# FFN 1 of a hybrid encoder layer on Trainium2: the norm factor moved from the activations to the gates, two more tiles in Strassen pairs, a bias write cut in pieces

## The chip, the cores and the metric

The kernel runs on one core of one Trainium2 chip. The metric is the device time of one launch in microseconds (us), the median of several runs. Beside it stands one profiled execution, of which the hardware profiler gives every instruction with its start and duration. The engines are TensorE (PE, with its weight loads as PEld), VectorE (DVE), ScalarE (ACT), GpSimd (POOL) and SyncE (SP). Each takes its own queue of instructions strictly in order; semaphores tie the queues together.

## The reference, cut to what matters

One layer, 512 tokens, width 1024, FFN width 2816, all float32:

```python
f = swiglu(rms_norm(x, ffn1_pre_g), ffn1_w1, ffn1_w3, ffn1_w2)   # (silu(u @ w1) * (u @ w3)) @ w2
h = x + 0.5 * rms_norm(f, ffn1_post_g)
u = rms_norm(h, mix_pre_g)
...   # RG-LRU branch, sliding-window attention with a relative bias, gates, w_o
h = h + rms_norm(merged @ w_o, mix_post_g)
f = swiglu(rms_norm(h, ffn2_pre_g), ffn2_w1, ffn2_w3, ffn2_w2)
h = h + 0.5 * rms_norm(f, ffn2_post_g)
```

`rms_norm(x, g) = x * r * g` with one factor `r = 1 / sqrt(mean(x^2) + eps)` for each token. The change concerns the first two lines only. The relative bias (16 heads) is needed in the attention, in the middle of the layer.

## The kernel before, in words

**Split products.** Each float32 operand is split into a high part (an ACT copy to fp32r) and a low part (a DVE subtraction), `hi` and `lo` (`split2`, L189; `split_to`, L149, for weights). A product of two split operands is three matmuls, hi·hi, lo·hi and hi·lo, into one PSUM bank. PE does little else than these.

**FFN 1, single tiles.** The 2816 columns of `w1a` and `w3a` are 22 tiles of 128 columns each. For the first `NC1 = 6` tiles a unit (`mm_feat`, L194) takes the eight 128-row pieces of x^T, three matmuls of 128x512 each, 24 in all. x^T is multiplied by the gain `g` alone and split into the tile `uT` (L665, L666). The factor r is not in it: it is computed from x meanwhile (L676 to L686), spread over the partitions by four small matmuls (L700) into `Rb`, and multiplied on each of the two results of a tile when the gate is made: `silu_mul` (L426) is two multiplications by `Rb` (L433, L434), a silu on ACT (L435), and the product (L436).

**FFN 1, pairs.** The other 16 tiles go two at a time through the class `Pairs` (L478): each pair of tiles and each of the two weights is a *job*, a 2x2 block product done with seven half-width block products instead of eight (Strassen's scheme in Winograd's form). A block product is `mm_s` (L466): twelve matmuls of 128x256. For this the weights need sums (`prep(m, 0)`, four POOL instructions L518 to L521) and splits (`prep(m, 1)` to `prep(m, 4)`, an ACT copy and a DVE subtraction each, L191 and L192), and the activations need four blocks and four sums of blocks, `X1`: `b11, b21, b22, t1` to `t4`, each split. Here x^T **with** the factor is used: `norm_x` (L770, L773) makes it with 16 DVE instructions while the single tiles run, `sums` makes the sums, and the splits go into slots or, as soon as the last single tile has read `uT`, into `uT` (L789 to L794). Inside a job, PSUM bank `bu` carries three successive sums: it is copied out by ACT as `q1` (L551) and as `u` (L560), and the next block product adds on top of it, so PE can't go on in `bu` before the ACT copy. The block product with `a22` is run one job later (`last`, L590), after the next job's second product; for a `w1a` job the silus of all four blocks follow there (L593, L594, L595).

The order of a job on PE is: a11·b11 (`bu`), s1·t1 (`bx`), the previous job's a22·t4, s2·t2 (`bu`), a12·b21 (`bc`), s4·b22 (`bx`), s3·t3 (`bu`). While job n runs, `prep` for job n+1 and the sums for n+2 are issued.

**Order of the work.** There is no scheduler. Each engine's queue is the order in which the Python code calls. `later(n, fn)` and `point()` (L175, L179) place work a number of *points* ahead: a point comes after half a unit, after each `mm_s`, and after each two token tiles in the last product. SP issues the weight loads in the order of the list `order`, each into a slot of a shared pool.

**Then** `tok_gemm` (L330) multiplies the 22 hidden tiles by `w2a`; each k-step is 24 matmuls of 128x512. Two broadcasts (`bcast`, L254, POOL queue) bring the gains near its end, and `norms` does the post norm (`post_norm`, L260, with `eps` as a constant), the residual and the next pre norm.

**The bias.** Two small loads on POOL's queue at the start (L651, L652), one matmul (L691), a copy (L693), and one DMA on POOL's queue (L696) that writes each of the 16 rows 128 times to a scratch in DRAM, 3064 KB. It is read back in the attention (L1012).

Of the kernel before, what the change touches and what calls it, by code (L numbers as in the profile page):

```python
# [51 lines left out]
def hybrid_layer(ctx: ExitStack, tc: tile.TileContext, a: dict, out: bass.AP):  # L52
# [32 lines left out]

    cp.tile([P, 176], F32, name="gap")
    sm.tile([P, 256], F32, name="gap2", bufs=1)
# [139 lines left out]
    class Rstd2:  # L227

        def first(self, ss):
            self.b, self.v, self.r, self.e, self.r2 = (small(1, x) for x in ("b", "v", "r", "e", "r2"))
            dve.tensor_scalar(out=self.b, in0=ss[:, 0:1], scalar1=D * EPS, scalar2=None, op0=ALU.add)

# [9 lines left out]
    def rstd4(s4):  # L244

        v, r, e, r2 = (small(NT, x) for x in ("v", "r", "e", "r2"))
        dve.tensor_scalar(out=v, in0=s4, scalar1=D * EPS, scalar2=None, op0=ALU.add)
        act.activation(r, v, AF.Abs_reciprocal_sqrt)
        dve.tensor_tensor(out=e, in0=r, in1=r, op=ALU.mult)
        dve.tensor_tensor(out=e, in0=e, in1=v, op=ALU.mult)  # L250
        dve.scalar_tensor_tensor(out=r2, in0=e, scalar=-3.0, in1=r, op0=ALU.add, op1=ALU.mult)
        return r2, r

# [5 lines left out]

    def post_norm(acc, t, gpost, scale, dst, after=None, last=False):  # L260

# [5 lines left out]
        for n, c in enumerate(cs):  # L267
            act.activation(junk[:, c], acc[n], AF.Square, accum_out=ss[:, n : n + 1])
            if n:
                rs.root(ss)  # L270
            dve.scalar_tensor_tensor(out=fg[:, c], in0=acc[n], scalar=scale, in1=gpost[:, c], op0=ALU.mult, op1=ALU.mult)
            if not n:
                rs.first(ss)
        r = rs.value()
# [6 lines left out]

    def norms(acc, t, gpost, scale, gpre, spill):

# [10 lines left out]

        post_norm(acc, t, gpost, scale * NEWT, h[t], half)
        if spill:
# [32 lines left out]

    def tok_gemm(nm, xs, n, R, gpost_name, scale, gpre_name, first, x_to=None, xf=None, spill=False, then=None):  # L330

# [36 lines left out]
        gpre = bcast(gpre_name) if gpre_name else None  # L368
        us, trs = {}, {}
        split_to(st["get"] + len(first))  # L370
        dma_to(st["split"] + 2)
        for t in range(NT):
# [15 lines left out]
            if t == NT - 2:  # L388

                transpose_out(trs[t - 1], t - 1)  # L390
            us[t] = norms(acc[t], t, gpost, scale, gpre, spill)
            if t == NT - 2 and xf:
# [7 lines left out]
        for i, key in enumerate(first):  # L400
# [11 lines left out]
            if i == 0:  # L412
                trs[t - 1] = transpose_mm(us[t - 1])
                us[t] = norms(acc[t], t, gpost, scale, gpre, spill)
                transpose_out(trs[t - 1], t - 1)
# [22 lines left out]

    class Hidden:


        def __init__(self):
            self.f, self.t, self.done = [], {}, 0
# [34 lines left out]
    class Pairs:  # L478

        def __init__(self, na, nb, f0, X, hid):
# [52 lines left out]
        def run(self, tail, hooks={}):  # L535
# [4 lines left out]
            for n, (nm, f) in enumerate(self.jobs):  # L540
# [49 lines left out]
                def last(W=W, bu=bu, c=c, f=f, first=first):  # L590
                    mm_s(W.pop("a22"), X["t4"], bu, True)
                    if first:
                        act.activation(c[:, 1, :256], bu, AF.Silu)  # L593
# [6 lines left out]

            last()


# [36 lines left out]
    dma_to(NS + 2)  # L640
    h_load([a["x"][t * P : (t + 1) * P, :] for t in range(NT)])

    hid, X1 = Hidden(), {}
    pairs_a = Pairs("w1a", "w3a", NC1, X1, hid)
    dma_one(pairs_a.k0)
# [29 lines left out]
    del raw3, pair3, hi, lo  # L675
    split_to(NS + 2)  # L676
    s4 = small(NT, "s4")
    for t in range(NT):
        junk = slot([P, D], name="junk")
        act.activation(junk, h[t], AF.Square, accum_out=s4[:, t : t + 1])  # L680

    r, q = rstd4(s4)
    act.activation(tiny, q, AF.Silu)
    dgs = slot([P, NT, P], name="dgs")
    for t in range(NT):
        dve.tensor_scalar(out=dgs[:, t, :], in0=ident, scalar1=r[:, t : t + 1], scalar2=NEWT, op0=ALU.mult, op1=ALU.mult)  # L686
    pairs_a.prep(0, 0, dve)
    ps.append(unit("w3a", 1))

    pse = bank("e")  # L690
    pe.matmul(pse[:N_HEADS, : NREL + 1], oh[:, NREL + 1 :], oh[:, : NREL + 1], start=True, stop=True)  # L691
    erow = slot([N_HEADS, NREL + 1], name="erow")
    act.activation(erow, pse[:N_HEADS, : NREL + 1], AF.Copy)  # L693
    scr = tc.dram_tile([N_HEADS, P, NREL], F32, name="bias_scr")
    ev = erow[:, :NREL]
    pool.dma_start(out=scr, in_=bass.AP(tensor=ev.tensor, offset=ev.offset, ap=[ev.ap[0], [0, P], ev.ap[1]]))  # L696
    Rb = slot([P, SEQ], name="Rb")
    psr = bank("r")
    for t in range(NT):
        pe.matmul(psr[:, t * P : (t + 1) * P], ones, dgs[:, t, :], start=True, stop=True)  # L700
    act.activation(Rb, psr, AF.Copy)
    pairs_a.prep(0, 1)
    hid.f += [silu_mul(ps[0], ps[1], Rb), silu_mul(ps[2], ps[3], Rb)]
    pairs_a.prep(0, 2)
    later(1, lambda: pairs_a.prep(0, 3))
    later(2, lambda: pairs_a.prep(0, 4))

# [27 lines left out]

    def swiglu_units(na, nb, f0, f1, hid, R=None):
        for f in range(f0, f1):
            p1, p3 = unit(na, f), unit(nb, f)
            later(1, lambda p1=p1, p3=p3: hid.f.append(silu_mul(p1, p3, R)))

    def uview(hh, th):
# [3 lines left out]
    def pair_view(p):  # L745
        return lambda e, k: p[e][:, k, :]

    def sums(xf):

        t = [slot([P, 4, 256], name="T") for _ in range(4)]  # L750
        pool.tensor_tensor(out=t[2], in0=xf[1, 1], in1=xf[0, 1], op=ALU.subtract)
        dve.tensor_tensor(out=t[0], in0=xf[0, 1], in1=xf[0, 0], op=ALU.subtract)
        dve.tensor_tensor(out=t[1], in0=xf[1, 1], in1=t[0], op=ALU.subtract)
        dve.tensor_tensor(out=t[3], in0=xf[1, 0], in1=t[1], op=ALU.subtract)
        return t

# [11 lines left out]
    xn, tn = {(hh, th): slot([P, 4, 256], name="xn") for hh in range(2) for th in range(2)}, []  # L768
# [8 lines left out]
    for k in range(KT):  # L777
        later(2 + k // 2, lambda k=k: norm_x(k))
    later(6, lambda: xts.clear())
    later(6, lambda: tn.extend(sums(xn)))  # L780
    later(7, lambda: X1.update(b11=to_slots(xn[0, 0])))
    later(9, lambda: X1.update(t1=to_slots(tn[0])))
    later(11, lambda: X1.update(t2=to_slots(tn[1])))
    end = 2 * 2 * (NC1 - 2)
    for i, at_ in enumerate((end - 5, end - 2, end - 1)):
        later(at_, lambda i=i: pairs_a.prep(1, i))
    swiglu_units("w1a", "w3a", 2, NC1, hid, Rb)
    point(True)
    X1["b21"] = to_uT(xn[1, 0], 1, 0)  # L789

    late = {
        (0, 1): [lambda: X1.update(b22=to_uT(xn[1, 1], 1, 1))],
        (0, 2): [lambda: X1.update(t3=to_uT(tn[2], 0, 1))],
        (0, 3): [lambda: X1.update(t4=to_uT(tn[3], 0, 0)), tn.clear, xn.clear],  # L794
    }

# [410 lines left out]

NC1 = 6
NC2 = 2
# [54 lines left out]
```

## Time and profile before

| | us |
|---|---|
| median of 3 runs (lowest, highest) | 1135.44 (1135.13, 1135.78) |
| the profiled execution's own time | 1135.67 |
| its span, first to last instruction | 1133.8 |
| first matmul of the paired stage of FFN 1 | 74.1 |
| first matmul of w2 of FFN 1 | 235.4 |

The span and the time differ by 1.87 us of work around it. The profiled execution lies 0.23 us above the median. In all tables "busy" is the time that an engine executes, and "idle before" is its wait ahead of an instruction with what ended it.

### The profile page before, as it was taken

To read this page: it belongs to the slowest core of one execution; us is meant where nothing else is said; L and a number is where in the kernel's file an instruction comes from. 1 tells how busy PE (TensorE), PEld (TensorE's weight loads), DVE (VectorE), ACT (ScalarE), POOL (GpSimd) and SP (SyncE) were. 2 spreads that over 40 slices of the span, in tenths; PEclk is the share of its full clock that TensorE was granted. 3 is DMA by queue.
4 is the path that set the end of the run, shared out by engine and by line. 5 is a ranking of instruction groups with operands and counts; after the bars stand their busy time and mean duration, and the time that the engine had idled before them with its cause. 6 is when DMAs were issued, how large, how long until landed. Compare 5 with 4: busy or idle time off the path is not lost.

```text
span 1133.8 us, 17339 instructions
## 1 busy us (share of the span) xinstructions
PE 1125.3 (99%) x6763; PEld 1003.5 (89%) x6763; DVE 790.1 (70%) x1181; ACT 585.2 (52%) x1042; POOL 353.8 (31%) x265
## 2 busy tenths in 40 slices
PE   9999999999999999999999999999999999999997
PEld 7889999988889987888888888889999999998886
DVE  5997889885436747695678865767899777975313
ACT  6445555574324349844655663356555555574211
POOL 0148678500000000001555643000965566700000
PEclk9999999999999999999999999999999999999999
DMA  9953223264313311234122333531323332255101
GB/s 343 157 135 112 93 95 112 76 222 151 110 56 135 144 56 57 75 95 148 56 78 90 93 95 112 185 111 38 113 94 94 112 112 76 94 197 172 40 19 56
DMA packets 36945, 124.94 MB, mean 110 GB/s; under 512 B 4416, under 2 KB 6208, under 8 KB 36864
## 3 DMA queue, kind: packets, MB, share of 16 engines
q1 hardware_dynamic: 34272, 115.15, 30.3%
q0 software_dynamic: 2448, 8.43, 4.0%
q8 instruction: 53, 0.87, 0.3%
q10 hardware_dynamic: 144, 0.26, 0.1%
q14 instruction: 28, 0.23, 0.1%
HBM read 116.50 MB, written 7.33 MB: 109 GB/s over the span
## 4 chain that ended last, share of the span: by engine, by line
PE 93%; DVE 3%; ACT 2%; issue 1%; DMA 0%; SPq 0%; DVEq 0%
PE c L475 11%; PE c L474 11%; PE c L473 11%; PE f L202 10%; PE f L201 10%; PE f L203 10%; PE acc L220 8%; PE acc L221 8%; PE acc L219 8%; PE pt L1067 1%; PE s L1031 1%; PE s L1030 1%; PE tr L310 1%; PE o L1083 1%; PE o L1084 1%
## 5 line engine op out<-in xcount | busy, mean ns | idle before, releaser
L201 PE MATMUL f<-uT,whi 128*128 128x512 f32 (+1 forms) x504 | 184.2, 365 | 0.0
L202 PE MATMUL f<-uT,wlo 128*128 128x512 f32 (+1 forms) x504 | 183.0, 363 | 0.4 <-DVE wlo L157 0.3
L203 PE MATMUL f<-uT,whi 128*128 128x512 f32 (+1 forms) x504 | 182.6, 362 | 0.0
L219 PE MATMUL acc<-whi,hT 128*128 128x512 f32 x352 | 137.1, 390 | 0.0
L220 PE MATMUL acc<-wlo,hT 128*128 128x512 f32 x352 | 137.0, 389 | 0.0
L221 PE MATMUL acc<-whi,hT 128*128 128x512 f32 x352 | 136.9, 389 | 0.0
L474 PE MATMUL c<-Xh,wlo 128*128 128x256 f32 x432 | 122.3, 283 | 0.0
L475 PE MATMUL c<-Xl,whi 128*128 128x256 f32 x432 | 122.3, 283 | 0.0
L473 PE MATMUL c<-uT,whi 128*128 128x256 f32 x432 | 122.3, 283 | 0.0
L474 PE MATMUL c<-uT,wlo 128*128 128x256 f32 x432 | 122.3, 283 | 0.0
L475 PE MATMUL c<-uT,whi 128*128 128x256 f32 x432 | 122.3, 283 | 0.0
L473 PE MATMUL c<-Xh,whi 128*128 128x256 f32 x432 | 122.3, 283 | 0.0
L192 DVE TENSOR_TENSOR wlo<-S,whi 128x1024 fp32r<-128x1024 f32 x72 | 118.2, 1642 | 3.6 <-ACT whi L191 3.2
L202 PEld LDWEIGHTS f<-uT,wlo 128*128 128x128 f32 x504 | 95.2, 189 | 15.8 <-DVE wlo L157 1.6
L201 PEld LDWEIGHTS f<-uT,whi 128*128 128x128 f32 x504 | 95.1, 189 | 15.8 <-issue 1.4
L203 PEld LDWEIGHTS f<-uT,whi 128*128 128x128 f32 x504 | 95.1, 189 | 14.8
L473 PEld LDWEIGHTS c<-Xh,whi 128*128 128x128 f32 x432 | 82.9, 192 | 0.0
L474 PEld LDWEIGHTS c<-Xh,wlo 128*128 128x128 f32 x432 | 82.9, 192 | 0.0
L473 PEld LDWEIGHTS c<-uT,whi 128*128 128x128 f32 x432 | 82.9, 192 | 0.0
L474 PEld LDWEIGHTS c<-uT,wlo 128*128 128x128 f32 x432 | 82.9, 192 | 0.0
L475 PEld LDWEIGHTS c<-uT,whi 128*128 128x128 f32 x432 | 82.9, 192 | 0.0
L475 PEld LDWEIGHTS c<-Xl,whi 128*128 128x128 f32 x432 | 82.9, 192 | 0.0
(309 smaller groups left out, 2703.8 us busy)
## 6 DMA issues: line engine op xcount, KB each, us to landing
raw_w2a<-in_w2a_dram SPq DMA_DIRECT2D x22, 512.0 KB, 3.7
raw_w1b<-in_w1b_dram SPq DMA_DIRECT2D x22, 512.0 KB, 4.2
raw_w3b<-in_w3b_dram SPq DMA_DIRECT2D x22, 512.0 KB, 4.2
raw_w2b<-in_w2b_dram SPq DMA_DIRECT2D x22, 512.0 KB, 4.1
raw_w3a<-in_w3a_dram SPq DMA_DIRECT2D x21, 512.0 KB, 4.5
raw_w1a<-in_w1a_dram SPq DMA_DIRECT2D x20, 512.0 KB, 4.5
raw_wg<-in_wg_dram SPq DMA_DIRECT2D x16, 512.0 KB, 3.7
raw_xr<-in_xr_dram SPq DMA_DIRECT2D x8, 512.0 KB, 4.7
```

Of the source, the lines that this page charges most:

```text
L192: dve.tensor_tensor(out=lo, in0=src, in1=f32(hi), op=ALU.subtract)
L201: pe.matmul(ps[:, c0:c1], wh[:, s], h_, start=k == 0, stop=False)
L202: pe.matmul(ps[:, c0:c1], wl[:, s], h_, start=False, stop=False)
L203: pe.matmul(ps[:, c0:c1], wh[:, s], l_, start=False, stop=k == KT - 1)
L219: pe.matmul(acc[n], x[:, 0, c], wh[:, s], start=first, stop=False)
L220: pe.matmul(acc[n], x[:, 0, c], wl[:, s], start=False, stop=False)
L221: pe.matmul(acc[n], x[:, 1, c], wh[:, s], start=False, stop=last)
L310: pe.transpose(ps[:, k * P : (k + 1) * P], hg[:, kk * P : (kk + 1) * P], ident)
L473: pe.matmul(ps, wh[:, s], xh, start=first, stop=False, skip_group_check=True)
L474: pe.matmul(ps, wl[:, s], xh, start=False, stop=False, skip_group_check=True)
L475: pe.matmul(ps, wh[:, s], xl, start=False, stop=k == 3, skip_group_check=True)
L1030: pe.matmul(o, lq, KS[g][:, 0, k0 : k0 + n], start=True, stop=False)
```

## The change

It makes the paired stage of FFN 1 work on the same unscaled `uT` as the single tiles. Blocks `b11, b21, b22` of `X1` are then plain views of `uT`; only the four sums are made (from `xg`, x^T times g, written by 16 ACT instructions) and split. The factor goes onto the w1 result alone, ahead of the silu; the w3 result stays without it. The hidden tile is then too large by 1/r for each token, which the post norm divides out if its `eps` is multiplied by the same ratio, so `post_norm` takes a column `veps` in place of the constant. `NC1` goes from 6 to 4: tiles 4 and 5 become a ninth pair. The work between is placed anew by hand, and the bias write is cut into eight pieces that are issued during w2.

```diff
-    def post_norm(acc, t, gpost, scale, dst, after=None, last=False):
+    def post_norm(acc, t, gpost, scale, dst, after=None, last=False, eps=D * EPS):
...
         if R is None:
             act.activation(t[:, 0, :], ps1, AF.Silu)
-            dve.tensor_tensor(out=t[:, 1, :], in0=ps3, in1=t[:, 0, :], op=ALU.mult)
         else:
             dve.tensor_tensor(out=t[:, 0, :], in0=ps1, in1=R, op=ALU.mult)
-            dve.tensor_tensor(out=t[:, 1, :], in0=ps3, in1=R, op=ALU.mult)
             act.activation(t[:, 0, :], t[:, 0, :], AF.Silu)
-            dve.tensor_tensor(out=t[:, 1, :], in0=t[:, 1, :], in1=t[:, 0, :], op=ALU.mult)
+        dve.tensor_tensor(out=t[:, 1, :], in0=ps3, in1=t[:, 0, :], op=ALU.mult)
...   # class Pairs, last()
-                    if first:
+                    if first and self.R is not None:
+                        act.activation(c[:, 1, :256], bu, AF.Copy)
+                        dve.tensor_tensor(out=c, in0=c, in1=self.R, op=ALU.mult)
+                        act.activation(c, c, AF.Silu)
+                    elif first:
                         act.activation(c[:, 1, :256], bu, AF.Silu)
                         act.activation(c[:, 0, :], c[:, 0, :], AF.Silu)
                         act.activation(c[:, 1, 256:], c[:, 1, 256:], AF.Silu)
...   # the start
-    oh = slot([N_BUCKETS, NREL + 1 + N_HEADS], name="oh")
-    pool.dma_start(out=oh[:, : NREL + 1], in_=a["onehot"])
-    pool.dma_start(out=oh[:, NREL + 1 :], in_=a["rel_bias"])
+    dma_to(NS + 3)          # one more single tile's load ahead of the first pair's
...
+    def scaled(k):
+        for th in range(2):
+            act.activation(xg[k // 4, th][:, k % 4, :], xts[k // 2][:, k % 2, th * 256 : th * 256 + 256], AF.Copy,
+                           scale=vec[:, V_G1 + k : V_G1 + k + 1])
+    def factor():
+        psr = bank("r")
+        for t in range(NT):
+            pe.matmul(psr[:, t * P : (t + 1) * P], ones, dgs[:, t, :], start=True, stop=True)
+        for i in range(2):
+            act.activation(Rb[:, i, :], psr, AF.Copy)
+    def bias_spread(i):
+        ev = erow[0][2 * i : 2 * i + 2, :NREL]
+        pool.dma_start(out=scr[2 * i : 2 * i + 2], in_=bass.AP(tensor=ev.tensor, offset=ev.offset, ap=[ev.ap[0], [0, P], ev.ap[1]]))
...
-    def norm_x(k):
-        for th in range(2):
-            c = slice(th * 256, th * 256 + 256)
-            dve.scalar_tensor_tensor(
-                out=xn[k // 4, th][:, k % 4, :], in0=xts[k // 2][:, k % 2, c],
-                scalar=vec[:, V_G1 + k : V_G1 + k + 1], in1=Rb[:, c], op0=ALU.mult, op1=ALU.mult)
...
+    X1.update((b, uview(*q)) for b, q in (("b11", (0, 0)), ("b21", (1, 0)), ("b22", (1, 1))))
+    P_ = pairs_a.prep
+    for n, fn in (
+        (1, lambda: t_sum(0)), (1, lambda: t_split(0)), (2, lambda: t_sum(1)),
+        (3, lambda: P_(0, 0, dve)), (3, lambda: t_split(1)), (3, squares), (4, root),
+        (5, lambda: P_(0, 1)), (5, lambda: t_sum(2)), (6, factor), (6, lambda: swiglu(0)), (6, lambda: dma_to(pairs_a.k0 + 4)),
+        (7, lambda: t_sum(3)), (7, lambda: t_split(2)), (8, lambda: P_(0, 2)), (8, lambda: swiglu(1)),
+        (9, lambda: P_(0, 3)), (9, lambda: P_(0, 4)), (10, lambda: t_split(3)), (10, lambda: swiglu(2)),
+        (10, lambda: P_(1, 0, dve)),
+    ):
+        later(n, fn)
...
+    swiglu(3)
+    late = {(6, 1): [bias_in], (9, 1): [bias_rows]}
...
+    for i in range(N_HEADS // 2):
+        later(4 + 3 * i, lambda i=i: bias_spread(i))
     later(10, softplus)
-    bs = tok_gemm("w2a", hid, FT, RF, "ffn1_post_g", 0.5, "mix_pre_g", [("xr", i) for i in range(4)], hid.to, spill=True)
+    bs = tok_gemm("w2a", hid, FT, RF, "ffn1_post_g", 0.5, "mix_pre_g", [("xr", i) for i in range(4)], hid.to, spill=True, eps=veps)
...
-NC1 = 6
+NC1 = 4
```

In the new file these lines stand a few lines lower: the new multiplication of a pair's block by the factor is L597 there, the copy ahead of it L596, the silu L598, and the gate's lines are L436 (factor), L437 (silu), L438 (product).

More of the change, by code (lines that the diff above doesn't have):

```diff
@@ L84, in hybrid_layer @@
     bxh = cp.tile([P, 2, KT], F32, name="bxh")
-    cp.tile([P, 176], F32, name="gap")
+    veps = cp.tile([P, NT], F32, name="veps")
+    cp.tile([P, 172], F32, name="gap")
     sm.tile([P, 256], F32, name="gap2", bufs=1)
@@ L227, in hybrid_layer, with first @@
     class Rstd2:
-        def first(self, ss):
+        def first(self, ss, eps=D * EPS):
             self.b, self.v, self.r, self.e, self.r2 = (small(1, x) for x in ("b", "v", "r", "e", "r2"))
-            dve.tensor_scalar(out=self.b, in0=ss[:, 0:1], scalar1=D * EPS, scalar2=None, op0=ALU.add)
+            dve.tensor_scalar(out=self.b, in0=ss[:, 0:1], scalar1=eps, scalar2=None, op0=ALU.add)
         def root(self, ss):
@@ L251, in rstd4 @@
         dve.scalar_tensor_tensor(out=r2, in0=e, scalar=-3.0, in1=r, op0=ALU.add, op1=ALU.mult)
-        return r2, r
+        dve.tensor_scalar(out=veps, in0=v, scalar1=EPS, scalar2=None, op0=ALU.mult)
+        return r2
     def bcast(name):
@@ L272, in post_norm @@
             if not n:
-                rs.first(ss)
+                rs.first(ss, eps)
         r = rs.value()
@@ L280, in post_norm, with norms @@
                 after(n, c)
-    def norms(acc, t, gpost, scale, gpre, spill):
+    def norms(acc, t, gpost, scale, gpre, spill, eps):
         hg = slot([P, D], name="hg")
@@ L293, in half @@
             dve.scalar_tensor_tensor(out=hg[:, c], in0=h[t][:, c], scalar=NEWT, in1=gpre[:, c], op0=ALU.mult, op1=ALU.mult)
-        post_norm(acc, t, gpost, scale * NEWT, h[t], half)
+        post_norm(acc, t, gpost, scale * NEWT, h[t], half, eps=eps)
         if spill:
@@ L327, in transpose_xf, with tok_gemm @@
             act.activation(xf[half, t // 2][:, :, (t % 2) * P : (t % 2 + 1) * P], v, AF.Copy)
-    def tok_gemm(nm, xs, n, R, gpost_name, scale, gpre_name, first, x_to=None, xf=None, spill=False, then=None):
+    def tok_gemm(nm, xs, n, R, gpost_name, scale, gpre_name, first, x_to=None, xf=None, spill=False, then=None, eps=None):
         F = n - R
@@ L369, in tok_gemm @@
         us, trs = {}, {}
+        ep = lambda t: D * EPS if eps is None else eps[:, t : t + 1]
         split_to(st["get"] + len(first))
@@ L390, in tok_gemm @@
                 transpose_out(trs[t - 1], t - 1)
[L391 removed]
+            us[t] = norms(acc[t], t, gpost, scale, gpre, spill, ep(t))
             if t == NT - 2 and xf:
@@ L675, in hybrid_layer @@
     del raw3, pair3, hi, lo
-    split_to(NS + 2)
-    s4 = small(NT, "s4")
[L678 to L693, printed above, removed]
-    scr = tc.dram_tile([N_HEADS, P, NREL], F32, name="bias_scr")
[L695 to L706, printed above, removed]
+    split_to(NS + 1)
+    xg, tg = {(hh, th): slot([P, 4, 256], name="xg") for hh in range(2) for th in range(2)}, {}
+    def scaled(k):
+        for th in range(2):
+            act.activation(xg[k // 4, th][:, k % 4, :], xts[k // 2][:, k % 2, th * 256 : th * 256 + 256], AF.Copy,
+                           scale=vec[:, V_G1 + k : V_G1 + k + 1])
@@ new lines, in t_sum, with t_split, squares @@
+    def t_sum(n):
+        tg[n] = slot([P, 4, 256], name="T")
+        p, q = ((xg[0, 1], xg[0, 0]), (xg[1, 1], tg.get(0)), (xg[1, 1], xg[0, 1]), (xg[1, 0], tg.get(1)))[n]
+        dve.tensor_tensor(out=tg[n], in0=p, in1=q, op=ALU.subtract)
+    def t_split(n):
+        X1[f"t{n + 1}"] = to_slots(tg[n])
+    dgs = slot([P, NT, P], name="dgs")
+    s4 = small(NT, "s4")
+    def squares():
+        for t in range(NT):
+            junk = slot([P, D], name="junk")
+            act.activation(junk, h[t], AF.Square, accum_out=s4[:, t : t + 1])
@@ new lines, in root @@
+    def root():
+        r = rstd4(s4)
+        act.activation(tiny, tiny, AF.Silu)
+        for t in range(NT):
+            dve.tensor_scalar(out=dgs[:, t, :], in0=ident, scalar1=r[:, t : t + 1], scalar2=NEWT, op0=ALU.mult, op1=ALU.mult)
+    def factor():
+        psr = bank("r")
+        for t in range(NT):
+            pe.matmul(psr[:, t * P : (t + 1) * P], ones, dgs[:, t, :], start=True, stop=True)
+        for i in range(2):
+            act.activation(Rb[:, i, :], psr, AF.Copy)
+    scr = tc.dram_tile([N_HEADS, P, NREL], F32, name="bias_scr")
@@ new lines, in hybrid_layer, with bias_in, bias_rows @@
+    oh, erow = [], []
+    def bias_in():
+        oh.append(slot([N_BUCKETS, NREL + 1 + N_HEADS], name="oh"))
+        pool.dma_start(out=oh[0][:, : NREL + 1], in_=a["onehot"])
+        pool.dma_start(out=oh[0][:, NREL + 1 :], in_=a["rel_bias"])
+    def bias_rows():
+        pse = bank("e")
+        t = oh.pop()
+        pe.matmul(pse[:N_HEADS, : NREL + 1], t[:, NREL + 1 :], t[:, : NREL + 1], start=True, stop=True)
+        erow.append(slot([N_HEADS, NREL + 1], name="erow"))
+        act.activation(erow[0], pse[:N_HEADS, : NREL + 1], AF.Copy)
@@ L734, in softplus @@
                     scalar1=0.5, scalar2=None, op0=ALU.mult)
[L736 to L739, printed above, removed]
     def uview(hh, th):
@@ L746, in pair_view @@
         return lambda e, k: p[e][:, k, :]
[L748 to L755, printed above, removed]
     def to_slots(src):
@@ L765, in to_uT @@
         return uview(hh, th)
-    xn, tn = {(hh, th): slot([P, 4, 256], name="xn") for hh in range(2) for th in range(2)}, []
-    def norm_x(k):
-        for th in range(2):
-            c = slice(th * 256, th * 256 + 256)
-            dve.scalar_tensor_tensor(
-                out=xn[k // 4, th][:, k % 4, :], in0=xts[k // 2][:, k % 2, c],
-                scalar=vec[:, V_G1 + k : V_G1 + k + 1], in1=Rb[:, c], op0=ALU.mult, op1=ALU.mult)
-    for k in range(KT):
-        later(2 + k // 2, lambda k=k: norm_x(k))
@@ L779, in hybrid_layer, with single @@
[L779 to L787, printed above, removed]
-    point(True)
[L789 to L795, printed above, removed]
+    def single(nm, i, ahead):
+        w = get(nm, i, ahead=ahead)
+        ps.append(bank("f"))
+        mm_feat(ps[-1], w)
@@ L797, in w2_ahead @@
+    for k in range(4):
+        scaled(k)
+    split_to(NS + 2)
+    for k in range(4, KT):
+        scaled(k)
+    xts.clear()
+    for u, ahead in zip(order[NS : 2 * NC1], [1] * (2 * NC1 - NS - 1) + [0]):
+        single(*u, ahead)
+    point(True)
+    xg.clear()
+    tg.clear()
+    swiglu(3)
+    late = {(6, 1): [bias_in], (9, 1): [bias_rows]}
     def w2_ahead():
```

12 lines of the change are left out of this document (8 added, 4 removed).

## The prediction

> **What bounds the kernel now.** I read the page's first part, then the waits of PE, then busy time by stage, then the timelines of ACT and DVE around one job of the paired stage.
>
> ```profile
> span 1133.8 us, 17339 instructions
> PE 1125.3 (99%) x6763; PEld 1003.5 (89%) x6763; DVE 790.1 (70%) x1181; ACT 585.2 (52%) x1042; POOL 353.8 (31%) x265
> ```
>
> The waits of PE over the whole span (total, times, longest) are two lines:
>
> ```profile
> PE w L625 <- DVE tiny L629: 1.4, 1, 1.4
> PE f L202 <- DVE wlo L157: 0.3, 1, 0.3
> ```
>
> So PE sets the time, and after the first microseconds it waits for nobody. A change gains what it takes off PE and loses every wait that it gives PE. Busy time by stage (end of the start to the paired stage, then the paired stage):
>
> ```profile
> 30.10:51.90 21.80, 21.80 (x98) 18.03 (x97) 20.73 (x34) 9.40 (x12) 2.83 (x2) 1.00 0.96 136
> 51.90:74.60 22.70, 22.40 (x101) 18.29 (x100) 20.83 (x20) 9.53 (x12) 7.91 (x5) 1.00 0.60 114
> 74.60:246.00 171.40, 171.40 (x1389) 169.59 (x1388) 144.14 (x150) 97.41 (x166) 106.69 (x56) 1.00 0.36 118
> ```
>
> The third number after the stretch is PEld, then come DVE, ACT and POOL. DVE is busy 93% from 30 to 75 us and 84% in the paired stage: it is the engine with no room where the change works. The paired stage of today, ACT first, then DVE:
>
> ```profile
> 84.40 0.38 ACT L551 ACTIVATE ct<-c 128x256 f32<-128x256 f32 x1 [0.54 <-PE c L475]
> ...
> 87.28 0.38 ACT L593 ACTIVATE cc<-c 128x256 f32<-128x256 f32 x1 [1.06 <-PE c L475]
> 87.56 0.62 ACT L594 ACTIVATE cc<-cc 128x512 f32<-128x512 f32 x1
> 88.08 0.41 ACT L595 ACTIVATE cc<-cc 128x256 f32<-128x256 f32 x1
> 88.39 1.05 ACT L191 ACTIVATE whi<-raw_w1a 128x1024 fp32r<-128x1024 f32 x1
> 89.34 0.38 ACT L560 ACTIVATE ct<-c 128x256 f32<-128x256 f32 x1
> ```
>
> ```profile
> 84.20 1.51 DVE L579 TENSOR_TENSOR cc<-ct 128x256 f32<-128x256 f32 x1
> 85.63 1.78 DVE L192 TENSOR_TENSOR w<-raw_w3a,w 128x512 fp32r<-128x512 f32 x1
> ...
> 90.94 2.31 DVE L192 TENSOR_TENSOR wlo<-S,whi 128x1024 fp32r<-128x1024 f32 x1
> ...
> 95.42 0.41 DVE L579 TENSOR_TENSOR cc<-ct 128x256 f32<-128x256 f32 x1
> ...
> 96.69 0.68 DVE L192 TENSOR_TENSOR w<-raw_w1a,w 128x512 fp32r<-128x512 f32 x1
> ```
>
> The same DVE instruction takes 0.41 or 1.51 us, 0.68 or 1.78: 1.1 more when one of POOL's sums, 1.3 us alone, is under way (POOL ran one from 83.27 to 85.43 and from 85.39 to 86.87). POOL's own go from 1.3 to 2.16. The two take turns, whole instructions at a time, wherever DVE reads two SBUF operands.
>
> **PE's own work.** A single unit is 24 matmuls of 128x512; the unit that starts at 22.71 ends its issue 0.2268 us a matmul later, 5.44 in all. A job is 84 matmuls of 128x256; L551 starts at 84.40, 94.48, 104.56: 10.08 a job, 0.120 a matmul, not half of 0.2268, since PEld is full there (169.59 of 171.40). Four units go (21.77), two jobs come (20.16): **1.61 saved**, where the count of columns (21 of 24) would promise 2.7. The bias matmul (0.74) only moves. The first 22.7 us stay, and the loads of w2 and all later stages keep their order.
>
> **The start.** Out go 16 `norm_x` on DVE (0.41 each) and three splits; in come 16 `scaled` copies on ACT (0.40 alone), hidden by 40% of idle ACT before 40 us. The gates lose L434, but it ran while ACT did the silu; without it DVE stands idle in its queue for that time (multiply at 32.90, silu at 33.62, product at 34.29, so 1.99 us a gate, as before). The paired stage now begins after five units instead of nine and the factor's four matmuls (0.92): 22.71 + 3 x 5.44 = 39.04, + 0.92 + 2 x 5.44 = 50.85, 23 us earlier, and its preparation has to be done by then. It is not. The factor is copied 1.2 us after its matmuls begin (28.98 to 30.18) and takes 0.60, so the first gate starts on DVE at about 40.9. From there the built DVE queue holds, up to the multiplication of the fourth gate: three gates (3 x 1.99 = 5.97), six instructions of 1024 columns at 1.14 apart (the low parts of the last single weight, S12, S34, t3 and t4, and the sum t4: 6.84), one of 512 (0.60), four weight sums of job 1 (4 x 0.60 and two hand-offs: 2.6), and two waits for a high part from ACT (0.35 each): 16.7 us. So 57.6; the silu starts 0.7 later. On ACT the copies of gates and jobs stand in one queue: the fourth silu is **ahead of** `q1` of job 0, which therefore is done at 58.3 + 0.53 + 0.38 = 59.2. PE needs `q1` before s2·t2, at 50.85 + 2 x 1.44 = 53.7. PE waits 5.5 us, or 6.7 where POOL's first sums, whose loads no longer meet the bias write, take a turn among the four DVE sums. I take **6.0**. Behind that silu also stands the first split of job 1; it is done two products later, inside PE's next 5.8 us.
>
> **The paired stage.** For each w1 job the three silus (0.38, 0.62, 0.41) become a copy, a DVE multiplication of 1024 columns (L597; L752 is such a one, 1.21) and a silu of 1024 (an ACT copy of that size takes 1.05, 0.95 to the next). Behind them on ACT stand the split of the next weight and `u` (L560), and PE can't begin s3·t3 before `u` is copied. Today `u` is done at 89.72; s3·t3 begins five products after 84.3, at 91.5: 1.8 us of room. With the change: 87.28 + 0.38, hand-off 0.06, DVE 1.22, hand-off 0.06, silu 0.95, split 0.95, copy 0.38 = 91.28. 0.2 us of room is left, if DVE is free and POOL is not in its turn. In today's trace DVE is free at that point of all eight jobs, by as little as 0.3 (w22 ends at 87.41), and POOL is in a sum in four of eight: a wait up to 1.3. Then all splits of the next job come 1.6 to 2 later on ACT; their low parts on DVE have 1.2 of room (the one of S12 ends at 93.25, s1·t1 of that job asks for it at 94.4). So a period of two jobs loses between 0 and 1.3 + 1.2. I walked all nine periods instruction by instruction in the order of the built queues, with these durations and POOL and DVE taking turns: 0.3 to 2.5 each, **11.0** in all. The same walk over the old queues gives PE no wait, as the trace has. With all durations of an engine 3% (POOL 7%) shorter or longer the sum is 8.6 to 14.9.
>
> **At nothing.** The eight spread issues (L696 took 1.03) hide in POOL's 78 us of idleness ahead of L257; the two small loads moved into job 6 stand ahead of POOL's sums there and cost it about 1.2, which the walk holds. `eps` as a column instead of a constant: same instruction, -0.1 to 0.1. The second copy of the factor (0.53 on ACT) lies ahead of the first silu, which waits for DVE anyway. The load order gives the third single tile 26.1 instead of 28.6 and job 0's weights 27.4 and 28.6; DVE sums them at 29.
>
> **Sum.** 1135.67 (profiled) - 1.6 + 6.0 + 11.0 = 1151.1; the median lies 0.2 lower: **1151**.
>
> **The rivals.**
> *PE's clock after the wait.* PE's first nine matmuls (L625) start 0.45 apart, twice 0.2268, and the pace doubles at 6 us: after idleness PE was slow for 4.5 us. No later gap in this trace shows whether 6 us of waiting suffice. If so, 4.5 us at half pace cost 2.2: 1153. 0.30. The Trainium skill ("TensorE: Matmul & The Clock Gate", Part 1) says that one idle window of about 3.4 us sets the clock to half; by that rule this case would hold, and this trace bears it out only at the start.
> *The start alone.* Small gaps on PE give POOL and DVE room, and the stage settles with the 0.2 of slack; at most 2 us in nine periods. 1135.5 - 1.6 + 6.0 + 1 = 1141. For it: POOL is idle in half the cases. Against: the room is 0.2 and the turn 1.3. 0.11.
> *Not slower: the fourth gate is not late.* If DVE gets from the first gate to the fourth in 12 us instead of 16.7, `q1` is free in time, and if the room of 0.2 then holds in all periods, only the pairing is left: 1133.9. Against: no row is that short. 0.04.
> *The pieces.* The one write moved 16 rows in 33.3 us:
>
> ```profile
> bias_scr<-erow POOLq DMA_DIRECT2D x1, 3064.0 KB, 33.3
> ```
>
> A piece has two rows. At the same pace for each row it takes up to 33 us, while one is issued every 8.2. Side by side they end at 101 us of w2, and the gains' broadcast, in the same queue, lands about 11 us later than PE asks for the first normed tile (at 94): 1162. One after the other they take 266, and PE waits 186. Against: w2's own loads need little of the engines (share 0.33), and fewer rows at a time should be faster each. 0.05. The Trainium skill ("DMA: Bandwidth & Descriptors", Rules for kernel authors) says that an outermost dimension of less than 16 confines a DMA to that many engines, so a piece would have two of 16; the write before had 16 rows, so no trace here shows it.
>
> **How the numbers follow.** The forecast as summed 0.48, with the slow clock 0.30, the start alone 0.11, the pieces 0.05, no wait 0.04, the rest (a gain that I don't see) 0.02. The range takes in the walk's 8.6 to 14.9, the start's 4.3 to 7.9 (same variation), the clock, and most of the start-alone case: 1140 to 1160. A measurement of this kernel tells 0.2%, 2.3 us, from no change: slower 0.94, same 0.04, faster 0.02.
>
> **What would show it.** In the profile after, PE's waits should list one of about 6 us at a `c` matmul with DVE or ACT (`ct` L554) near 54 us, and many of 0.3 to 2 us in the paired stage, released by ACT L563 (`u`) and DVE's low parts; L597 should last 1.2 to 2.5; the paired stage should start at 51 and w2 at about 251 instead of 235.4. Wrong, if w2 starts before 240, or if the loss lies in w2 or later.

## The result, and the profile after

The kernel after takes 1168.39 us (median of 6 runs, 1168.14 to 1169.88), the one before 1135.45 in the same measurement: 1.0293 times as long (95% interval 1.0279 to 1.0306). Slower was right; 33 us instead of the forecast 15.5 lies outside the range. The profiled execution took 1168.26, so it stands for the median.

The top of the page, to be held against the two lines of before:

```profile
span 1166.2 us, 17529 instructions
PE 1131.0 (97%) x6835; PEld 1010.4 (87%) x6835; DVE 799.4 (69%) x1180; ACT 595.5 (51%) x1060; POOL 360.6 (31%) x275
```

PE is no longer busy all the time. What it waited for (total, times, longest):

```profile
PE c L475 <- ACT ct L581: 12.9, 1, 12.9
PE c L475 <- ACT ct L554: 8.6, 4, 7.6
PE c L475 <- ACT ct L563: 3.3, 6, 1.2
PE c L476 <- DVE wlo L194: 1.6, 5, 0.5
```

The second to fourth lines are the waits that the prediction had: `q1` (L554) at the start (the 7.6), `u` (L563) and the low parts in the paired stage. The first was in no sum. L581 is the copy `v` of a job, and it happens once, for 12.9 us. Busy time by stage says where (the paired stage's first 24 us, the rest of it, the last job):

```profile
50.46:74.00 23.54, 15.95 (x114) 15.74 (x113) 15.02 (x18) 7.93 (x14) 8.98 (x7) 0.78 0.25 89
74.00:250.00 176.00, 170.16 (x1381) 166.19 (x1380) 149.30 (x147) 91.42 (x150) 115.12 (x67) 1.00 0.31 93
250.00:267.00 17.00, 4.11 (x25) 3.91 (x24) 4.52 (x8) 1.51 (x3) 0.00 (x0) 0.61 0.93 163
```

PE's busy time is the second number, the granted clock the third from the end, the DMA engines' share the one behind it. The paired stage began at 50.45 (forecast 51), w2 at 266.99 (forecast 251, before 235.40). In the last job PE worked 4 of 17 us, at a clock of 0.61, while the DMA engines were 93% busy. The ACT queue of that stretch, then POOL's:

```profile
249.56 0.62 ACT L193 ACTIVATE hT<-sw 128x512 fp32r<-128x512 f32 x1
262.88 1.06 ACT L158 ACTIVATE whi<-raw_w2a 128x1024 fp32r<-128x1024 f32 x1 [12.70 <-DMA raw_w2a<-in_w2a_dram]
263.84 0.36 ACT L581 ACTIVATE ct<-c 128x256 f32<-128x256 f32 x1
```

```profile
235.38 1.74 POOL L524 TENSOR_TENSOR S<-raw_w3a,raw_w3a 128x512 f32<-128x512 f32 x1
237.07 7.42 POOL L741 DMA_DIRECT2D bias_scr<-erow  x7
271.66 1.07 POOL L741 DMA_DIRECT2D bias_scr<-erow  x1 [27.16 <-DMA bias_scr<-erow]
```

Read from the bottom. Seven of the eight bias pieces left POOL in 7.4 us, 1.05 apart, right behind the last weight sum and 30 us before w2. The code calls for them at points of w2, but a point only says where in POOL's queue an instruction stands. Nothing on that queue waits for w2, the row copy was long done, and so they went. These seven took 34 to 48 us to land; the eighth could leave only when the first had landed. Beside them the load of the second w2 tile, issued at 241.05, landed at 262.86. From issue to landing that load took (after, then before):

```profile
raw_w2a<-in_w2a_dram SPq DMA_DIRECT2D x1, 512.0 KB, 21.8
```

```profile
raw_w2a<-in_w2a_dram SPq DMA_DIRECT2D x1, 512.0 KB, 3.7
```

ACT's split waited for it, with `v` behind it in the queue, and PE waited for `v`.

### The profile page after: what moved, and what is told of

It is laid out like the page before. It is cut to its first block, busy times and chain, and to the rows that moved or that the text cites. A ratio compares the mean times of both kernels' runs of the same rounds, so it can differ in the third digit from the quotient of the medians.

```text
span 1166.2 us, 17529 instructions
## 1 busy us (share of the span) xinstructions
PE 1131.0 (97%) x6835; PEld 1010.4 (87%) x6835; DVE 799.4 (69%) x1180; ACT 595.5 (51%) x1060; POOL 360.6 (31%) x275
## 2 busy tenths in 40 slices
DMA packets 41873, 125.00 MB, mean 107 GB/s; under 512 B 9344, under 2 KB 11136, under 8 KB 41792
## 4 chain that ended last, share of the span: by engine, by line
PE 80%; DVE 7%; DMA 5%; ACT 5%; issue 2%; SPq 0%; DVEq 0%; ACTq 0%
PE f L204 9%; PE f L203 9%; PE f L205 9%; PE c L475 8%; PE c L476 8%; PE c L477 8%; PE acc L223 8%; PE acc L221 8%; PE acc L222 8%; DVE wlo L194 3%; DMA raw_w2a<-in_w2a_dram 2%; ACT whi L193 1%; DVE cc L597 1%; PE pt L1093 1%; DMA raw_w3a<-in_w3a_dram 1%
## 5 line engine op out<-in xcount | busy, mean ns | idle before, releaser
L203 PE MATMUL f<-uT,whi 128*128 128x512 f32 (+1 forms) x472 | 171.9, 364 | 0.0
L204 PE MATMUL f<-uT,wlo 128*128 128x512 f32 (+1 forms) x472 | 170.7, 362 | 0.1
L205 PE MATMUL f<-uT,whi 128*128 128x512 f32 (+1 forms) x472 | 170.4, 361 | 0.0
L475 PE MATMUL c<-Xh,whi 128*128 128x256 f32 x456 | 131.0, 287 | 11.8 <-ACT ct L554 8.6
L476 PE MATMUL c<-Xh,wlo 128*128 128x256 f32 x456 | 130.3, 286 | 1.6 <-DVE wlo L194 1.6
L476 PE MATMUL c<-uT,wlo 128*128 128x256 f32 x456 | 129.8, 285 | 0.0
L475 PE MATMUL c<-uT,whi 128*128 128x256 f32 x456 | 129.8, 285 | 0.0
L477 PE MATMUL c<-Xl,whi 128*128 128x256 f32 x456 | 129.7, 285 | 0.0
L477 PE MATMUL c<-uT,whi 128*128 128x256 f32 x456 | 129.6, 284 | 0.0
L203 PEld LDWEIGHTS f<-uT,whi 128*128 128x128 f32 x472 | 89.2, 189 | 14.5 <-issue 1.4
L204 PEld LDWEIGHTS f<-uT,wlo 128*128 128x128 f32 x472 | 89.3, 189 | 13.7 <-DVE wlo L159 0.9
L205 PEld LDWEIGHTS f<-uT,whi 128*128 128x128 f32 x472 | 89.2, 189 | 13.5
L475 PEld LDWEIGHTS c<-Xh,whi 128*128 128x128 f32 x456 | 88.0, 193 | 14.7 <-ACT ct L554 10.2
L476 PEld LDWEIGHTS c<-Xh,wlo 128*128 128x128 f32 x456 | 88.1, 193 | 2.6 <-DVE wlo L194 2.6
L476 PEld LDWEIGHTS c<-uT,wlo 128*128 128x128 f32 x456 | 88.2, 193 | 0.2 <-DVE wlo L194 0.2
L475 PEld LDWEIGHTS c<-uT,whi 128*128 128x128 f32 x456 | 88.2, 194 | 0.0
L477 PEld LDWEIGHTS c<-uT,whi 128*128 128x128 f32 x456 | 88.1, 193 | 0.0
```

Of the source, the lines that this page charges most:

```text
L203: pe.matmul(ps[:, c0:c1], wh[:, s], h_, start=k == 0, stop=False)
L204: pe.matmul(ps[:, c0:c1], wl[:, s], h_, start=False, stop=False)
L205: pe.matmul(ps[:, c0:c1], wh[:, s], l_, start=False, stop=k == KT - 1)
L475: pe.matmul(ps, wh[:, s], xh, start=first, stop=False, skip_group_check=True)
L476: pe.matmul(ps, wl[:, s], xh, start=False, stop=False, skip_group_check=True)
L477: pe.matmul(ps, wh[:, s], xl, start=False, stop=k == 3, skip_group_check=True)
```

## The experiments

All kernels are edits of the kernel after, but for one that edits the kernel before.

**The pieces held back.** Ahead of each piece POOL reads the newest hidden tile:

```diff
+    def held(i, hid):
+        n = f32(hid.t[hid.done - 1][:, 0, 0:4])
+        pool.tensor_tensor(out=small(4, "hold"), in0=n, in1=n, op=ALU.add)
+        bias_spread(i)
-        later(4 + 3 * i, lambda i=i: bias_spread(i))
+        later(4 + 3 * i, lambda i=i, hid=hid: held(i, hid))
```

> The eight pieces stay pieces, but ahead of each one POOL now reads the newest hidden tile, so a piece can't leave before w2 has got that far. Theory A (place: nothing on POOL's queue held the pieces, seven left at 237 to 243 and met w2's first loads): the 12.9 us wait for `v` and the half clock behind it (about 3) go, w2's first matmul at 251 instead of 267, 1152.4. If the pieces, one each 8 us in w2, slow w2's loads there a little: up to 1156. Theory B (shape: two rows in a piece make a slow, many-packet transfer that harms the loads wherever it lies): the wait moves into w2, 1162 to 1168. Theory C (w2's loads are late for a reason of their own): nothing changes, 1168.

1159.96 us (1.0213, 1.0195 to 1.0230). The 12.9 us are gone; w2 began at 254.24. But a wait of 4.2 us stands in w2 now, with 6.8 us at half clock from there on. It is for a hidden tile's high part, which stands in ACT's queue behind splits of four loads that landed 12 to 25 us after issue. Place and shape both count. (In this profiled run the start wait is 9.0 instead of 7.6: three of DVE's sums met a POOL sum, not two.)

**One whole write in the same place, and one in the middle of the paired stage.**

```diff
-    def bias_spread(i):
-        ev = erow[0][2 * i : 2 * i + 2, :NREL]
-        pool.dma_start(out=scr[2 * i : 2 * i + 2], in_=...)
+    def bias_spread():
+        ev = erow[0][:, :NREL]
+        pool.dma_start(out=scr, in_=...)
...   # the first kernel: later(4, bias_spread); the second:
-    late = {(6, 1): [bias_in], (9, 1): [bias_rows]}
+    late = {(6, 1): [bias_in], (9, 1): [bias_rows, bias_spread]}
```

> One write of all 16 rows, as in the kernel before, at the place of the first piece; it leaves at 237 too. Theory A (place): the loads of w2 issued beside it land late all the same, PE waits 10 to 16 us ahead of w2, 1165 to 1170. Theory B (shape): the loads land in about 9 us, as the loads beside the one write of before did at 30 to 63 (8.8), no wait over 2 us, 1152 to 1155. Theory C: 1168.

1170.11 us (1.0303, 1.0288 to 1.0318), the wait for `v` 13.5. So it isn't the cutting that hurts there.

> One write of all 16 rows right behind the row copy in job 9 of the paired stage, about 155 us, where each load is issued three jobs (30 us) ahead of its use. Theory A: it lasts 33 us, loads beside it 9 us instead of 4.4, nobody waits for them; the 12.9 us wait and the half clock behind it go, 1152.4, w2 at 251. Theory B says the same here, theory C 1168. If POOL's queue waits for the row copy and its weight sums come late, 1 to 3 us more.

1171.12 us (1.0314, 1.0299 to 1.0329). Theories A and B said 1152, and C kept the wait ahead of w2; all were wrong. That wait is gone, and PE waited 17.8 us in job 11 instead. The DMA lines of the two, over the time of the write (size, median us to landing):

```profile
raw_w2a<-in_w2a_dram SPq DMA_DIRECT2D x9, 512.0 KB, 21.8
bias_scr<-erow POOLq DMA_DIRECT2D x1, 3064.0 KB, 35.6
```

```profile
bias_scr<-erow POOLq DMA_DIRECT2D x1, 3064.0 KB, 35.5
raw_w1a<-in_w1a_dram SPq DMA_DIRECT2D x2, 512.0 KB, 25.9
raw_w3a<-in_w3a_dram SPq DMA_DIRECT2D x2, 512.0 KB, 22.7
```

Loads that are issued beside the write take some 20 us more, here too. My "9 us" in the expectations came from a median in the profile of before that mixed loads issued well ahead of the write with loads beside it. Asked for the one load issued at 33.01, 2.7 us behind the write, the trace of before had said it all along:

```profile
raw_w3a<-in_w3a_dram SPq DMA_DIRECT2D x1, 512.0 KB, 23.4
```

Before, PE lost nothing of that size by it: its one wait there was 0.3 us. The 17.8 us in the middle of the paired stage have another cause, which the name of the releaser shows. ACT first, then POOL:

```profile
194.42 1.06 ACT L193 ACTIVATE whi<-S 128x1024 fp32r<-128x1024 f32 x1 [22.25 <-DMA bias_scr<-erow]
195.38 0.37 ACT L581 ACTIVATE ct<-c 128x256 f32<-128x256 f32 x1
```

```profile
194.08 1.26 POOL L521 TENSOR_TENSOR S<-raw_w1a 128x512 f32<-128x512 f32 x1 [24.39 <-DMA raw_w1a<-in_w1a_dram]
```

`v` (L581), which PE waits for, stands behind a split that waits for the write itself: the write landed at 194.34, while the sums that the split reads (`S`) were done at 169.70. The tile `whi` of that split takes the slot of `erow`, from which the write reads (both have the same address in the built program), so it can't be filled before the write is done. The late load held up POOL's sum for the job behind. What that alone would have cost PE, this run doesn't show; so it says that loads beside the write land late, but not that they cost the 17.8.

**The pieces alone, on the kernel before.** The one write goes, the eight two-row pieces come at the same points of w2; nothing else is changed.

> The kernel before with one part of the change alone: the eight two-row pieces in place of the one write, called for in w2 as the change has it. Theory A: POOL's last sum ends at 218.7 there, so seven pieces leave at once from 218.7 to 225, beside w2's first loads, which take 20 to 28 us instead of 3.5 to 6; w2 begins 8 to 14 us late with a half clock behind it: 1144 to 1152. Rival (the kernel before has room enough, the pieces hurt only with the new paired stage): 1135 to 1137.

1148.18 us (1.0114, 1.0100 to 1.0127): the seven pieces left from 219.51 on, PE waited 10.5 us for `v` of the last job, w2 began 12.1 late. This part of the change costs 13 us by itself (before took 1135.20 beside it), with the old paired stage too.

**Cut the other way.** As the first experiment, but each piece has 16 of the 128 copies of all 16 rows:

```diff
-        ev = erow[0][2 * i : 2 * i + 2, :NREL]
-        pool.dma_start(out=scr[2 * i : 2 * i + 2], in_=...[ev.ap[0], [0, P], ev.ap[1]])
+        ev = erow[0][:, :NREL]
+        pool.dma_start(out=scr[:, 16 * i : 16 * i + 16, :], in_=...[ev.ap[0], [0, 16], ev.ap[1]])
```

> As e1_held, but a piece has 16 of the 128 copies of all 16 rows, where e1's has all copies of two rows; same bytes, same eight moments in w2. Theory A (a two-row piece keeps about 2 of the 16 DMA engines for 23 to 37 us, and every load, which needs all engines, waits for those): a piece over all engines lasts 33.3 / 8 = 4.2 us, loads beside it are 4 to 5 us later instead of up to 24, the 4.2 us wait in w2 of e1_held and the half clock behind it (about 1.6) go: about 1153. Rival (bytes of this write are slow, the cut doesn't matter): as e1_held, 1159 to 1160.

1153.37 us (1.0161, 1.0147 to 1.0174), as theory A had it. PE has no wait in w2, and from w2's first matmul to the first transpose it takes 100.67 us, as before. The DMA lines from 250 to 320 us of the two-row pieces, then of these:

```profile
raw_w2a<-in_w2a_dram SPq DMA_DIRECT2D x17, 512.0 KB, 17.2
bias_scr<-erow POOLq DMA_DIRECT2D x8, 383.0 KB, 34.2
```

```profile
raw_w2a<-in_w2a_dram SPq DMA_DIRECT2D x17, 512.0 KB, 7.5
bias_scr<-erow POOLq DMA_DIRECT2D x8, 383.0 KB, 7.7
```

Same bytes, same points, a quarter of the time for each piece and less than half for the loads. From 310 to 317 us three two-row pieces were under way and the packets of POOL's DMA queue kept 34% of the 16 engines busy, 1.8 engines each. The rule that the prediction took from the Trainium skill ("DMA: Bandwidth & Descriptors", Rules for kernel authors), two rows outermost means two engines, is borne out by that. The two runs also differ in the number of small packets (under 512 bytes 9344 with the two-row pieces, 4528 with these); no run separates that from the number of engines.

**The fourth gate behind `u` of the first job.**

```diff
-    swiglu(3)
-    late = {(6, 1): [bias_in], (9, 1): [bias_rows]}
+    late = {(6, 1): [bias_in], (9, 1): [bias_rows], (0, 3): [lambda: swiglu(3)]}
```

> The fourth gate goes behind `u` of the first job, so its silu no longer stands ahead of `q1` on ACT. Theory A (ACT's queue order makes the start wait of 7.6 us, and that wait makes the half clock of 56 to 66 us, 2.5): the wait falls to about 3 in several parts (DVE is full there), none long enough for the clock, 1168.4 - 4.5 - 2.5 = 1161.4. Rival (DVE, not ACT's order, sets it): the same wait comes at the next tile that DVE is late with, 1166 to 1168. If the half clock comes without a long wait too: 1164.

1163.64 us (1.0247, 1.0232 to 1.0263), 4.8 less. The wait at 53 falls from 7.6 to 0.7. Three others of 1.3, 0.7 and 0.9 come at 60 to 65 us, for low and high parts that DVE and ACT are late with, and the granted clock stays at 1.00. So ACT's order made the wait long, and DVE, which is full there, keeps 3.6 us of it.

**The silu of the paired stage behind `u`.**

```diff
                         dve.tensor_tensor(out=c, in0=c, in1=self.R, op=ALU.mult)
-                        act.activation(c, c, AF.Silu)
+                        self.silu = lambda: act.activation(c, c, AF.Silu)
...   # in the next job, and self.silu starts as a function that does nothing
                 act.activation(u, bu, AF.Copy)
+                self.silu()
+                self.silu = lambda: None
```

> In the paired stage the one silu of 1024 columns goes behind `u` of the next job on ACT; copy and multiplication stay where they are. Theory A (the silu that waits for L597 on DVE holds up the split and `u` behind it): of the paired stage's waits, some 8.5 us in nineteen pieces, all but 2 to 3 go: 1168.4 - 6 = 1162.4. Rival (DVE itself, with one more instruction of 1024 columns and POOL's turns, is late whatever ACT's order): most stay, 1166 or more.

1161.49 us (1.0230, 1.0216 to 1.0244), 6.9 less. From `q1` of the second job to that of the last it takes 163.3 us instead of 171.6, and of the fourteen small waits that the list of after has (six at L563, five at L476, three of the four at L554) one of 0.6 is left. (The expectation's 8.5 us in nineteen pieces is not what that list has: fourteen with 5.8 us in sum. Some of the 8.3 is given back in w2, where a hidden tile now comes 0.8 and 0.6 late.)

**Is the half clock real?** 54 matmuls that nobody reads fill PE's wait for `q1`:

```diff
+                if n == 0:
+                    for _ in range(54):
+                        pe.matmul(banks[2][:, 256:], W["s1"][0][:, :P], uT[:, 0, 0, :256], start=True, stop=True, ...)
                 last()
```

> The kernel after with 54 matmuls of 128x256 that nobody reads, put on PE between s1·t1 and s2·t2 of the first job, where PE waits 7.6 us for `q1`: some 6.5 us of work into a wait. Theory A (PE's clock falls to half because PE stood idle, and that costs about 2.5 us at 56 to 66): the wait shrinks to about 1, the clock stays at 1.0 there, the paired stage goes on 2.5 earlier, 1165.9: PE does more and the kernel is faster. Rival (the clock falls for another reason, or the half clock there costs nothing that isn't hidden): 1168.4, or up to 1170 where the filler outlasts the wait.

1172.92 us (1.0337, 1.0323 to 1.0351). A mistake of mine: the first job of FFN 2 took the filler too. Next, FFN 1 alone.

> f1_filler with its mistake mended: the filler's condition held for the first job of FFN 2 as well, where PE waits for nothing and 54 matmuls cost their 6.5 us. Now they are in FFN 1 alone. Theory A (idleness makes the half clock at 56 to 66): f1 began w2 2.0 us before the kernel after, and after its extra 6.5 us in FFN 2 is taken off it gives 1166.4; so 1166.2 here. Rival (the clock's price there is hidden or the filler does harm): 1168.4 or more.

1169.92 us, but from 1166.09 to 1171.93. The profiled execution is the shortest. The stretch from 56 to 66 us of after, then of this one (the clock is the number 1.00 or 0.50):

```profile
56.00:66.00 10.00, 4.92 (x23) 4.92 (x24) 6.57 (x7) 4.07 (x7) 5.69 (x4) 0.50 0.13 38
```

```profile
56.00:66.00 10.00, 9.04 (x75) 8.84 (x75) 7.83 (x9) 4.40 (x7) 5.54 (x4) 1.00 0.18 57
```

With PE kept busy the clock stays up, and the second job's `q1` is copied at 68.39 instead of 70.72, 2.3 earlier, though PE did 6.5 us more work.

> f2_filler's five times lie from 1166.1 to 1171.9, so that its median says nothing of 2 us; the long wait ahead of w2 hangs on how the loads land beside the write. Here the same filler stands in e7_cut16, which has no such wait (1153.4). Theory A (standing idle for 7 us takes PE's clock to half, and that costs 2.2): 1151.2, w2's first matmul at 250.2 instead of 252.5. Rival (no price): 1153.4.

1152.89 us, again in two groups (1151.3, 1151.7 and 1154.1, 1154.5), against 1153.37. The profiled execution is the longest: three of DVE's sums met POOL's, the filler ended 2.4 us before `q1` was there, and the clock fell to half for 3.4 us all the same. So the traces show the price, 2.3 us, and what causes it; the times, which hang on POOL's turns too, don't confirm it by themselves.

**All three causes taken out.** The gate, the silu and the 16-row pieces together:

> e4_gate_j0, e5_silu and e7_cut16 together. Theory A (three separate causes: order on ACT at the start, order on ACT in the paired stage, the write beside the loads): before's 1135.7, less 2.8 (the paired stage began at 50.45 instead of 74.13, 23.68 earlier, for two jobs of 10.08 and the bias matmul of 0.74 more), plus e4's start waits of about 4.0, plus 0.9 left in the paired stage (e5), plus 0.4 behind w2: 1138.2. Rival (the parts share a cause, DVE being full, so that the small waits come back once the long ones, in which DVE catches up, are gone): 1142 or more.

1140.07 us (1.0046, 1.0032 to 1.0060), 28.3 less than after; 1.9 more than the sum said. Singly the three gave 4.8, 6.9 and 15.0, which is 26.7: the gains add up, and of the small waits in the paired stage only one of 0.6 is there, so they did not come back as the rival had it. Then with a second gate moved and the second job's sums on POOL:

```diff
-        (9, lambda: P_(0, 4)), (10, lambda: t_split(3)), (10, lambda: swiglu(2)),
-        (10, lambda: P_(1, 0, dve)),
+        (9, lambda: P_(0, 4)), (10, lambda: t_split(3)), (10, lambda: P_(1, 0)),
...
+    late = {..., (0, 3): [lambda: swiglu(2)], (1, 3): [lambda: swiglu(3)]}
```

> e8_three with two gates instead of one behind the start (the third behind `u` of the first job, the fourth behind `u` of the second) and the four weight sums of the second job on POOL, not DVE. Theory A: DVE gets 5 us of work less ahead of the first job, PE waits 1 us or less before 70 us: 1138.2 - 3 = 1135.2, level with the kernel before; all waits gone would give 1133. Rival (POOL's sums take DVE's turns, the waits only move): 1138 to 1140.

1136.61 us (1.0016, 1.0007 to 1.0025), 1.3 above the kernel before. What PE still waits for:

```profile
PE w L636 <- DVE tiny L640: 1.4, 1, 1.4
PE c L476 <- DVE wlo L194: 0.9, 1, 0.9
PE c L475 <- ACT ct L554: 0.6, 1, 0.6
...
```

The first is that of before's first microseconds. Mended as far as I got, the change costs about what it gains. No version ran faster than the kernel before.

## Why the prediction was wrong, step by step

By steps of the trace, in us (before's span 1133.8, after's 1166.2):

| step | forecast | measured | from |
|---|---|---|---|
| PE's own work | -1.6 | -2.8 | paired stage of 18 jobs at 10.08 and the bias matmul (0.7) from 50.45: w2 at 232.6, not 235.4 |
| start wait | 6.0 | 7.6 | PE's wait for `q1` |
| half clock after it | rival, 2.2 | 2.2 | second job's `q1` 20.27 behind the stage's start (70.72 - 50.45), with two gates moved 10.66 with 0.14 of waiting in it: 9.75 late, less 7.6 |
| small waits, nine periods | 11.0 | 10.1 | 171.6 from the second job's `q1` to the last job's, less 16 jobs of 10.08 and the bias matmul: 9.6; and 0.5 for a wait in the last job |
| the pieces | 0 (rival, 0.05) | 14.3 | after against the 16-row pieces: 1166.2 - 1151.3 in span, less 0.6, since the second job's `q1` came 20.27 behind the stage's start in the one and 19.62 in the other |

They add to 31.4 of the 32.4. Of the rest 0.4 lies behind w2's first matmul, with the 16-row pieces too (898.8 us to the end, before 898.4); 0.6 stays open.

**The step that failed** is the price of the pieces: nothing in the sum, since the issues hide in POOL's 78 us of idleness ("At nothing"), where 14.3 us were lost, and in the rival "the pieces" the clause "one is issued every 8.2". I took the point at which the code calls for an instruction for the time at which it runs. I looked for nothing on POOL's queue that waits, though those 78 us of idleness are themselves the sign of a queue with nothing in it to wait for. The last clause of the rival failed too: w2's loads "need little of the engines (share 0.33)". A share says nothing of how long one load takes when every engine is held by another queue. And the harm that the rival looked for, a late broadcast of the gains, is not the one that came.

**Mis-sized.** The start: its larger value, 6.7, was the case in which POOL's sums take a turn among DVE's, and that is the case that came, with two such turns (2.0 us more in sum), where 6.7 pays for 1.2. Two sums of DVE took 1.63 and 1.74 instead of 0.68, as these lines show, and the fourth gate's silu stands right ahead of `q1`:

```profile
56.19 1.63 DVE L523 TENSOR_TENSOR S<-raw_w3a,S 128x512 f32<-128x512 f32 x1
57.75 1.74 DVE L524 TENSOR_TENSOR S<-raw_w3a,raw_w3a 128x512 f32<-128x512 f32 x1
```

```profile
60.13 0.63 ACT L437 ACTIVATE sw<-sw 128x512 f32<-128x512 f32 x1 [6.02 <-DVE sw L436]
60.66 0.36 ACT L554 ACTIVATE ct<-c 128x256 f32<-128x256 f32 x1
```

PE's own work: 1.2 us more was saved, since the five units and the factor ended 0.4 earlier than reckoned and the nine units of before took 0.8 more than nine times 5.44 and the two extras. A reading was off as well: ACT was busy 27.5 of the first 40 us, so 31% idle, not 40%; the sixteen `scaled` copies didn't delay the units all the same.

**Right.** The paired stage: 10.1 for 11.0, by the mechanism that was named: eleven of the fourteen small waits are for `u` and for low parts, three for `q1`. The waits as listed sum to 5.8 only. At each such place PE loses 0.26 more: at the one below, two matmuls start 0.79 and then 0.22 apart instead of 0.12, which is 0.77, for a listed wait of 0.51. Here is a `w1` job with the multiplication (L597, 2.01 us in POOL's turn) between the copy (L596) and the silu (L598), and the split and `u` (L563) behind them:

```profile
94.64 0.38 ACT L596 ACTIVATE cc<-c 128x256 f32<-128x256 f32 x1 [1.06 <-PE c L477]
97.10 1.06 ACT L598 ACTIVATE cc<-cc 128x1024 f32<-128x1024 f32 x1 [2.07 <-DVE cc L597]
98.06 1.04 ACT L193 ACTIVATE whi<-raw_w1a 128x1024 fp32r<-128x1024 f32 x1
99.01 0.36 ACT L563 ACTIVATE ct<-c 128x256 f32<-128x256 f32 x1
```

PE's matmul that needs `u` (99.01 + 0.36) started at 99.43, 0.67 late. The slow clock, a rival at 0.30, came true twice: behind the start wait (half from 56 to 66 us), and behind the wait for `v`, where it is part of the 14.3. The Trainium skill ("TensorE: Matmul & The Clock Gate", Part 1) says that an idle window of about 3.4 us sets the clock to half. Both waits, 7.6 and 12.9 us, agree. With the write out of the way the forecast with that rival, 1153, is what the 16-row pieces measured: 1153.37. That it comes so close is luck in part: the terms were off by -1.2, +1.6 and -0.9, which nearly cancel.

## What to carry to other kernels

A place in the program is a place in a queue, not a time: before moving a DMA to "where there is room", find what on its own queue will hold it until then, and if nothing does, it leaves as soon as the queue is empty. Cost a big transfer by the landing of the single loads issued while it ran, never by their median, and set that against the time from issue to first use of the loads it will meet. Look also for who waits for the transfer itself: a tile that takes the place of its source has to. An activation that waits for another engine delays everything behind it in its queue: put it behind the copy that the next product needs.

## What was unexpected of the hardware

- Two rows took as long as sixteen: the one write of 3064 KB landed in 33.3 us, a two-row piece of 383 KB in 23 to 40 us (held back) or 32 to 48 us (seven at once). With 16 rows in each, a piece took 6 to 8 us.
- A load of 512 KB beside the whole write took 22 to 29 us instead of 3.5 to 6 where it was issued 3 to 15 us behind the write, and 30 us behind it still 12.
- In the kernel with the filler and the 16-row pieces, 2.4 us of waiting were enough to take PE's clock to half for 3.4 us; waits of up to 1.3 us in the gate experiment left it at 1.00. The Trainium skill ("TensorE: Matmul & The Clock Gate", Part 1) speaks of an idle window of about 3.4 us; the measurement lies below it.
- Nearly the same start wait brought half clock of different length: 10.2 us in the kernel after (7.6 us of waiting), 6.8 us with the 16-row pieces (7.4 us of waiting).
